# Modulation columns of the first layer's MLP: the context vector's dot products by GpSimd and ScalarE instead of VectorE

## The chip, the cores and the metric

The kernel runs on one core of a Trainium2 chip. The metric is device time in microseconds (us) of one execution; three runs of the kernel before gave 3952.34 to 3956.1, median 3953.94. TensorE multiplies matrices, VectorE (DVE), ScalarE (ACT) and GpSimd (POOL) work elementwise, and SyncE (SP) issues all DMAs. Each engine takes its instructions strictly in the order of the built program; semaphores make one engine wait for another.

## The reference, cut to what matters

Two layers of a diffusion backbone work on 1024 latent tokens and 256 context tokens of 1024 features. Each layer has a modulation: six times 1024 values for the latent tokens from the vector `c`, and six times 1024 for the context tokens from `c_ctx`, with the same weights.

```
sc, scc = silu(c), silu(c_ctx)
mod   = sc  @ w_ada[i] + b_ada[i]     # sh1, sc1, g1, sh2, sc2, g2, 1024 each
mod_c = scc @ w_ada[i] + b_ada[i]     # the same six for the context
...
x  = x  + g2  * squared_relu_mlp(modulate(x,  norm2_g, sh2,  sc2),  w_ff1, w_ff2)
xc = xc + cg2 * squared_relu_mlp(modulate(xc, norm2_g, csh2, csc2), w_ff1, w_ff2)
```

`squared_relu_mlp(h)` is `square(relu(h @ w_ff1)) @ w_ff2` with 4096 hidden features. The last layer computes no context output, so its context modulation beyond shift and scale of the first norm is not needed.

## The kernel before

Features lie on the 128 partitions, tokens along the free axis, in three blocks: block 0 is the context (256 tokens), blocks 1 and 2 the latent tokens (512 each). A weight [128, 1024] is loaded in float32 by `wload` (L296 on) and split into a high part (`whi`, ScalarE cast, L307) and its remainder (`wlo`, GpSimd subtraction, L308); every product is three matmuls (`mm3`, L313 to L315). Three such weights are held at a time.

The MLP of stage 3 is a loop over 16 steps, `fi` from 0 to 15, of two hidden tiles each. A step first makes six hidden tiles (`ff1`: matmuls into `fps`; `relu` and its square `ah` on ScalarE, L1290 and L1291; the square again in full precision on GpSimd, L1292; the remainder `al` on VectorE, L1293), then 24 output tiles (`ff2`: matmuls into `f2ps`; VectorE adds them to the residual times the gate `g2`, L1304). The gate for block 0 is that of the context. In step 0 the output tiles of block 0 come first. Matmul results share six PSUM banks, and a bank is free when ScalarE (`fps`) or VectorE (`f2ps`) has read it.

Beside the first layer's MLP the kernel computes the modulation that is still missing: column tile `m` (128 of the 6144 values, one per partition) is a dot product of a [128, 1024] piece of `w_adaT` with `silu(c)`, held on all partitions (`scr0`), and for some columns with `silu(c_ctx)` too (`scr1`). `ada_tile` (L257) does it in two halves: it loads a weight tile `adaw` of [128, 512] (256 KB, three buffers) and, for each vector, runs one VectorE instruction that multiplies and sums along the row (`adaj`, L272, followed by a short one that reads the accumulator). Step 0 lists the eight columns of `g2` of this layer (m = 40 to 47, both vectors); steps 1 to 12 list four columns each of the next layer (m = 0 to 47; both vectors up to m = 15, that is in steps 1 to 4). That is 112 weight tiles: 48 wanted for both vectors, then 64 for one, 160 VectorE instructions. A scheduler orders each engine's instructions when the program is built; it puts these tiles well ahead of the steps that list them.

`ada_tile` knows another way for vectors in its argument `other`: GpSimd multiplies (`adap`, L267, two buffers), ScalarE sums along the row into a table `part` (L268), and after eight columns `ada_sum` (L276) adds the two halves and the bias on VectorE (L279, L280). Earlier in stage 3, beside the output projection, eight columns take that way for the context vector.

Of the kernel before, what the change touches and what calls it, by code (L numbers as in the profile page):

```python
# [46 lines left out]
# columns of the constant table  # L47
C_ID, C_M0, C_M1, C_ONE, C_W = 0, 128, 256, 384, 512
# and the part of it that is needed once
# [24 lines left out]
def host_layout(inp):  # L74
    a = {k: np.asarray(v) for k, v in inp.items()}
    o = {}
    o["xT"] = np.concatenate([a["ctx"][0], a["x"][0]], 0).T.reshape(KD, P, NT).transpose(1, 0, 2)
    cc = np.stack([a["c"][0], a["c_ctx"]], 0)
    o["ccT"] = cc.reshape(2, KD, P).transpose(2, 1, 0)
    o["w_ada0"] = a["w_ada"][0, :, :2 * D]  # L80
    o["w_adaT"] = a["w_ada"].transpose(0, 2, 1)
    vec = [a["b_ada"].reshape(L * 48, P), a["norm1_g"].reshape(L * KD, P), a["norm2_g"].reshape(L * KD, P),
           a["final_norm_g"].reshape(KD, P)]
    o["vec"] = np.concatenate(vec, 0).T
    o["qag"] = a["q_a_g"].reshape(L, 2, P).transpose(0, 2, 1)
    o["kvg"] = a["kv_a_g"].reshape(L, P, 1)
    w = a["w_in"]
    q_a, kv_a, k_r, qkv, z, aa, bb = np.split(w, np.cumsum([256, 128, 32, 1536, 512, 8]), axis=-1)
    pad, pad2 = np.zeros((L, D, 48), np.float32), np.zeros((L, D, 16), np.float32)
    misc = np.concatenate([aa, bb, pad, k_r[..., :16], pad2, k_r[..., 16:], pad2], -1)  # L90
    # tiles of output columns: q 4, k 4, v 4, misc, kv_a, q_a 2, z 4
    cols = np.concatenate([qkv, misc, kv_a, q_a, z], -1)
    o["w_in"] = cols.reshape(L, KD, P, W_MT, P).transpose(0, 3, 2, 1, 4).reshape(L, W_MT, P, D)
    wq = a["w_q_b"].reshape(L, 256, H_A, DQK)
    nope = wq[..., :64].reshape(L, 256, 512)
    # the rotary columns: first halves of all heads, second halves of all heads
    pe = wq[..., 64:].reshape(L, 256, H_A, 2, 16).transpose(0, 1, 3, 2, 4)
    wq = np.concatenate([nope, pe.reshape(L, 256, 256)], -1)
    o["w_qb"] = wq.reshape(L, 2, P, QB).transpose(0, 2, 1, 3).reshape(L, P, 2 * QB)
    wk = a["w_kv_b"].reshape(L, P, H_A, 128)  # L100
    o["w_kvb"] = np.concatenate([wk[..., :64].reshape(L, P, 512), wk[..., 64:].reshape(L, P, 512)], -1)
    o["conv_w"] = a["conv_w"].reshape(L, 5, 12, P).transpose(0, 3, 2, 1).reshape(L, P, 60)
    o["a_log"] = a["a_log"].reshape(L, 8)
    o["dt_bias"] = a["dt_bias"].reshape(L, 8)
    o["gng"] = a["gdn_norm_g"].reshape(L, P, 1)
    o["w_out"] = a["w_out"].reshape(L, KD, P, KD, P).transpose(0, 3, 2, 1, 4).reshape(L, KD, P, D)
    o["w_ff1"] = a["w_ff1"].reshape(L, KD, P, 32, P).transpose(0, 3, 2, 1, 4).reshape(L, 32, P, D)
    o["w_ff2"] = a["w_ff2"].reshape(L, 32, P, D)
    tab, rope = host_constants()
    o["ctab"] = tab  # L110
    o["rope"] = rope
    return {k: np.ascontiguousarray(v) for k, v in o.items()}
# [3 lines left out]
class K:  # L116
# [13 lines left out]
    # ---------------------------------------------------------------- set-up  # L130
# [24 lines left out]
    def side(self, l):  # L155
        """The ends of the memory for the features and weights, and for the rest; layers swap them."""
        self.msd, self.osd = ("right", "left") if l % 2 else ("left", "right")
# [8 lines left out]
    def start(self, mmp, pjp, tpp, stp):  # L166
        """Modulation of the first norm, the first norm, and the first two output tiles, as the features come."""
        nc, io, cst = self.nc, self.io, self.cst
        with ExitStack() as es:
# [12 lines left out]
            # features and weights are queued behind the modulation's weights  # L182
# [10 lines left out]
            behind = START  # L193
# [62 lines left out]
    # ---------------------------------------------------------------- adaLN  # L256
    def ada_tile(self, l, m, vs, sp, width, other=()):  # L257
        """Column m of the modulation; the vectors in other go by way of Pool and ACT and want their sum()."""
# [17 lines left out]
    def ada_sum(self, l, v, m):  # L276
        """Eight columns that came by way of Pool and ACT, from their halves and the bias."""
# [4 lines left out]
    def load_sc(self, sp):  # L282
        """silu(c) and silu(c_ctx) on all partitions."""
# [6 lines left out]
    def gain(self, l, j, vs):  # L290
        """(1 + scale) * gain of norm j."""
# [5 lines left out]
    # ---------------------------------------------------------------- weights  # L297
    def wload(self, src):
        """A [128, 1024] weight from DRAM as its float32r high part and exact remainder."""
# [17 lines left out]
    # ---------------------------------------------------------------- norms  # L317
    def rstat(self, sq, n, denom, stp, rbp=None):
        """rsqrt(mean + eps) over partitions of the [128, n] squares (list added), as PSUM [128, n] rows."""
# [17 lines left out]
    def norm_mod(self, xs, rb, b, l, which, pool):  # L337
        """Modulated RMSNorm of block b (8 tiles [128, n]) into the high and low parts of h."""
# [22 lines left out]
    # ---------------------------------------------------------------- stage 1  # L361
    def stage1(self, l, last):
        """Input projection, short conv, gates, chunk preparation, latent attention's projections."""
# [8 lines left out]
        # the solves may go on into the next stage  # L372
# [59 lines left out]
        def conv_tile(m, blocks, it=None):  # L432
            """Projection, short conv, twice the silu."""
# [65 lines left out]
        def first():  # L499
            """The first two output tiles, side by side, while the norm goes on."""  # L500
# [72 lines left out]
    def kpe(self, l, it, sp, tpp):  # L573
        """Rotary key part of all heads, and the gate columns by token."""
# [40 lines left out]
    def gates(self, l, stp):  # L615
        """Per-token scalars of both directions, [128 tokens, direction, tile, head]."""
# [45 lines left out]
        # the squares are of twice the features  # L662
# [24 lines left out]
    # ---- latent attention's low-rank parts  # L687
# [6 lines left out]
    def lowrank(self, raw, b, g, sp, stp):  # L694
        """RMSNorm of the low-rank features of block b, as high and low parts."""
# [27 lines left out]
    def kv_proj(self, l, raw, sp, mmp, stp):  # L723
        """Keys (but for the rotary part) and values of all heads, to DRAM as high and low parts."""
# [20 lines left out]
    def q_proj(self, l, raw, sp, mmp, stp):  # L745
# [3 lines left out]
        # the scale of the scores  # L749
# [31 lines left out]
    # ---------------------------------------------------------------- stage 2  # L781
    def stage2(self, l, last):
        dr = self.dr
        es = ExitStack()
        # what the first scores need, and then the first steps, lies where the stage before ends first
# [4 lines left out]
        # the first scores wait for the products before them, not for the last transposes' banks  # L790
# [26 lines left out]
    def attention(self, l, last, ap, psA, psO):  # L817
# [4 lines left out]
        def parts(hi, lo, src):  # L822
            """Loads [p, n] or [p, t, n] values as their high and low parts."""
# [29 lines left out]
        # two units' results share a bank  # L853
# [3 lines left out]
        def front(h, b, half):  # L857
# [18 lines left out]
            def keep(i, c, s, c0, c1):  # L876
                """Takes scores out of their bank, with their maximum."""
# [3 lines left out]
            # the last 256 keys of both query tiles share a bank  # L881
# [18 lines left out]
            # by way of memory, to lie along the queries in all partitions  # L900
# [58 lines left out]
    def delta(self, l, last, gp, psG):  # L959
# [8 lines left out]
        # zero but for the blocks that each step fills  # L968
# [21 lines left out]
        def inverse(s):  # L990
            """The step's unit-triangular inverses, transposed, of both directions side by side: the blocks that they
            miss at each level lie in other rows and columns, so one product gives all of them."""
            U = [Ut[d, s % 2] for d in range(2)]
            B = Bt[s % 2].rearrange("p h (k j) -> p h k j", j=32)
            # at a level, direction d takes columns of blocks 2 i + d to rows of blocks 2 i + 1 - d; products of 32
            # lie in the four quarters of one of 64, a row group's right factor in the half of its parity
# [7 lines left out]
            def block(d, g, inv):  # L1004
                """Diagonal block g of the inverse (inv) or of its transpose."""
# [156 lines left out]
    # ---------------------------------------------------------------- stage 3  # L1162
    def stage3(self, l, last):
# [48 lines left out]
        for m0 in range(0, KD, 2):  # L1212
            # the last two tiles go block by block, so that the norm of a block runs beside the next one's products
# [31 lines left out]
        if not last:  # L1245
            adp = ad.enter_context(self.pool(f"ad_{l}", side=self.osd))
            self.load_sc(adp)
            ada = [(0, m, range(2)) for m in range(40, 48)] if l == 0 else []
            ada += [(l + 1, m, range(2 if m < 16 else 1)) for m in range(48)]
        # the pieces of the last products and of the norm after them  # L1250
# [28 lines left out]
        def ff1(w, b, cols=None):  # L1279
            """Squared relu of one tile, as high and low parts, by the given columns."""  # L1280
# [26 lines left out]
        for fi in range(nf):  # L1307
# [6 lines left out]
            # the last of them waits until the first block's end is under way  # L1314
# [4 lines left out]
            for a in ada[8 * fi:8 * fi + 8] if fi == 0 else ada[4 * fi + 4:4 * fi + 8]:  # L1319
                self.ada_tile(*a, adp, 512)  # L1320
# [37 lines left out]
class NormAcc:  # L1358
    """Running elementwise sum of the squares of [128, n] tiles."""
# [17 lines left out]
class Prep:  # L1377
    """Chunk preparation of the delta rule: decayed grams and inverses of the diagonal 32-blocks."""
# [57 lines left out]
    def a_view(self, d, s):  # L1436
        """The gram of a step, [row, head, column]; heads lie one block diagonal apart."""
# [3 lines left out]
    def solve(self, bi, sp):  # L1441
        """Unit-triangular inverses of the diagonal blocks of some steps, one block to a partition."""
# [4 lines left out]
        # lb[j, i] is the block's element (i, j); direction 1 holds it the other way round  # L1447
# [20 lines left out]
        # by step, head and row: blocks of the two directions in turn, each and its transpose  # L1468
# [23 lines left out]
```

## Time and profile before

| | |
|---|---|
| runs (three) | 3952.34, 3953.94, 3956.1 us |
| profiled execution, first to last instruction (span) | 3929.9 us |
| what lies around the span, against the median | 24.0 us |
| TensorE busy | 3517.4 us, 90% |
| VectorE busy | 2134.2 us, 54% |
| ScalarE busy | 1459.3 us, 37% |
| GpSimd busy | 1516.0 us, 39% |

The profiled execution's own time is given as its span alone; the time of a run has launch and end around it. Busy times are unions over the whole span, so a share says little of one stage: the MLP of the first layer runs from about 1245 us to 2121 us, and its first four steps are where the modulation is computed. Windows below are in us from the start of the span.

### The profile page before, as it was taken

The numbers are of one execution on the slowest core, as the hardware profiler recorded it, in microseconds if no ns is written. First come the engines' busy times: TensorE is split into PE (matmuls) and PEld (weight loads), VectorE is DVE, ScalarE is ACT, GpSimd is POOL, SyncE is SP. The second block draws the span as 40 slices with busy tenths as digits, with TensorE's granted clock in tenths as the row PEclk, the third lists the DMA queues.
The fourth block names the chain that finished last, engine by engine and source line by source line (L and its number), as shares of the span: only waits on it lengthen the run. The fifth ranks groups of instructions, "written<-read, shape, count | busy, mean of one in ns | idle before, by whom it ended". The sixth has DMA issues, their size and how long they took to land.

```text
span 3929.9 us, 52618 instructions
## 1 busy us (share of the span) xinstructions
PE 3517.4 (90%) x19001; PEld 2992.1 (76%) x19001; DVE 2134.2 (54%) x4080; ACT 1459.3 (37%) x3156; POOL 1516.0 (39%) x1358
## 2 busy tenths in 40 slices
PE   8789977887887898999999978888889899999998
PEld 4668766787776777888888757767788788888887
DVE  5157855565769995333333627776667533333334
ACT  4334355565633111121112524336666531222122
POOL 3124864433354232232223313675533352333232
PEclk8899987898998899999999979989899899999999
DMA  5343465535353352111111334454653511111111
GB/s 186 91 136 116 139 149 94 112 93 95 77 199 102 129 180 81 43 44 38 38 33 43 102 94 132 144 147 109 125 101 81 132 57 46 52 51 49 44 54 54
DMA packets 335892, 372.52 MB, mean 95 GB/s; under 512 B 126849, under 2 KB 226577, under 8 KB 333969
## 3 DMA queue, kind: packets, MB, share of 16 engines
q1 hardware_dynamic: 335632, 369.18, 34.3%
q8 instruction: 149, 2.44, 0.3%
q14 instruction: 111, 0.90, 0.1%
HBM read 280.65 MB, written 88.42 MB: 94 GB/s over the span
## 4 chain that ended last, share of the span: by engine, by line
PE 57%; DVE 13%; DMA 12%; issue 5%; ACT 4%; POOL 3%; SPq 1%; POOLq 0%; DVEq 0%; ACTq 0%
PE f2ps L313 6%; PE f2ps L314 6%; PE f2ps L315 6%; PE fps L314 6%; PE fps L315 6%; PE fps L313 6%; DVE adaj L272 3%; DMA raw<-kd 3%; PE g L984 3%; PE o L916 3%; PE pt L924 2%; DVE cacc L444 2%; DVE A L1427 2%; DMA rinv<-rinv 2%; DMA adaw<-w_adaT 1%
## 5 line engine op out<-in xcount | busy, mean ns | idle before, releaser
L308 POOL TENSOR_TENSOR wlo<-wraw,whi 128x1024 fp32r<-128x1024 f32 (+1 forms) x190 | 462.3, 2441 | 1217.8 <-ACT whi L307 1217.8
L1304 DVE SCALAR_TENSOR_TENSOR x<-f2ps,mod,x 128x512 f32<-128x512 f32 (+1 forms) x648 | 440.9, 689 | 353.3 <-PE f2ps L315 353.1
L307 ACT CAST whi<-wraw 128x1024 fp32r<-128x1024 f32 (+1 forms) x190 | 195.6, 1046 | 1008.0 <-PE f2ps L314 692.7
L313 PE MATMUL f2ps<-ah,whi 128*128 128x512 f32 (+1 forms) x1296 | 474.4, 371 | 31.4 <-DVE x L1304 27.2
L314 PE MATMUL f2ps<-al,whi 128*128 128x512 f32 (+1 forms) x1296 | 478.5, 370 | 0.8 <-DVE al L1293 0.8
L313 PE MATMUL fps<-hh,whi 128*128 128x512 f32 (+1 forms) x1288 | 471.3, 368 | 8.8 <-ACT hh L351 8.8
L315 PE MATMUL f2ps<-ah,wlo 128*128 128x512 f32 (+1 forms) x1296 | 477.4, 369 | 0.0
L314 PE MATMUL fps<-hl,whi 128*128 128x512 f32 (+1 forms) x1288 | 474.1, 368 | 0.0
L315 PE MATMUL fps<-hh,wlo 128*128 128x512 f32 (+1 forms) x1288 | 472.9, 368 | 0.0
L1293 DVE TENSOR_TENSOR al<-relu,ah 128x256 fp32r<-128x256 f32 (+1 forms) x161 | 111.5, 699 | 512.9 <-POOL relu L1292 512.9
L313 PE MATMUL mm<-hh,whi 128*128 128x512 f32 (+1 forms) x880 | 333.1, 380 | 35.0 <-ACT craw L430 22.1
L314 PE MATMUL mm<-hl,whi 128*128 128x512 f32 (+1 forms) x880 | 331.4, 377 | 3.6 <-DVE hl L352 2.1
L315 PE MATMUL mm<-hh,wlo 128*128 128x512 f32 (+1 forms) x880 | 327.6, 374 | 0.8 <-POOL wlo L308 0.8
L928 DVE TENSOR_TENSOR pl<-pt,ph 128x512 fp32r<-128x512 f32 x328 | 222.2, 686 | 194.7 <-ACT ph L927 182.1
L313 PEld LDWEIGHTS f2ps<-ah,whi 128*128 128x128 f32 x1296 | 248.2, 192 | 74.4 <-DVE x L1304 29.9
L313 PEld LDWEIGHTS fps<-hh,whi 128*128 128x128 f32 x1288 | 243.7, 190 | 49.1 <-ACT hh L351 9.1
L314 PEld LDWEIGHTS f2ps<-al,whi 128*128 128x128 f32 x1296 | 248.7, 192 | 40.7 <-DVE al L1293 1.0
L315 PEld LDWEIGHTS f2ps<-ah,wlo 128*128 128x128 f32 x1296 | 248.4, 192 | 40.1
L314 PEld LDWEIGHTS fps<-hl,whi 128*128 128x128 f32 x1288 | 244.0, 189 | 40.1 <-POOL hl L357 0.3
L315 PEld LDWEIGHTS fps<-hh,wlo 128*128 128x128 f32 x1288 | 243.9, 189 | 39.8
L924 PE MATMUL pt<-ctab,p 128*128 128x128 f32 x1312 | 219.9, 287 | 32.9 <-ACT p L896 12.7
L1292 POOL TENSOR_TENSOR relu<-relu 128x256 f32<-128x256 f32 (+1 forms) x161 | 159.5, 996 | 225.2 <-ACT ah L1291 209.7
(287 smaller groups left out, 7520.6 us busy)
## 6 DMA issues: line engine op xcount, KB each, us to landing
wraw<-w_ff SPq DMA_DIRECT2D x128, 512.0 KB
adaw<-w_adaT SPq DMA_DIRECT2D x160, 256.0 KB
wraw<-w_in SPq DMA_DIRECT2D x40, 512.0 KB
QK<-QK SPq DMA_DIRECT2D x72, 256.0 KB
A<-A SPq DMA_DIRECT2D x40, 256.0 KB
v<-vtd SPq DMA_DIRECT2D x40, 256.0 KB
kt<-ktd SPq DMA_DIRECT2D x40, 256.0 KB
kT<-kTd SPq DMA_DIRECT2D x36, 256.0 KB
```

The source lines that it names most:

```text
L272: nc.vector.tensor_tensor_reduce(out=j, in0=w, in1=self.sc_b[v][:, s], op0=ALU.mult, op1=ALU.add, scale=1.0, scalar=acc if i else self.bad ...
L307: nc.scalar.copy(hi[:, :n], raw[:, :n])
L308: nc.gpsimd.tensor_tensor(lo[:, :n], raw[:, :n], hi[:, :n].bitcast(F32), op=ALU.subtract)
L313: then(mm(ps, lhsT=lh, rhs=rh, start=start, stop=False))
L314: then(mm(ps, lhsT=lh, rhs=rl, start=False, stop=False))
L315: then(mm(ps, lhsT=ll, rhs=rh, start=False, stop=stop))
L916: nc.tensor.matmul(o, lhsT=v[:, k, :], rhs=x[:, j, :], start=k == 0 and i == 0, stop=k == nkt - 1 and i == 1)
L924: self.mark = nc.tensor.transpose(tp[:, j, i * P:(i + 1) * P], pp[i][:, (k0 + j) * P:(k0 + j + 1) * P], self.ident)
L928: nc.vector.tensor_tensor(pl, tp, ph.bitcast(F32), op=ALU.subtract)
L984: nc.tensor.matmul(ps[:, h, :], lhsT=lhs[:, h, :], rhs=rhs[:, h, :], start=True, stop=True)
L1292: nc.gpsimd.tensor_tensor(r[:, :n], r[:, :n], r[:, :n], op=ALU.mult)
L1304: nc.vector.scalar_tensor_tensor(xs, ps[:, :n], g2, xs, op0=ALU.mult, op1=ALU.add)
```

## The change

In the first layer's MLP loop every column is computed with `other=(1,)`: where a column is wanted for both vectors, the context's dot products go by GpSimd (48 products of [128, 512]) and ScalarE (48 sums). After each eighth such column (m = 47, then 7 and 15 of the next layer) `ada_sum` fills eight columns of the context's modulation. The latent vector's dot products stay on VectorE. Other differences are comments.

```
@@ stage3
             w2 = [self.wload(io["w_ff2"][l, f]) for f in fs]
             for a in ada[8 * fi:8 * fi + 8] if fi == 0 else ada[4 * fi + 4:4 * fi + 8]:
-                self.ada_tile(*a, adp, 512)
+                self.ada_tile(*a, adp, 512, (1,))
+                if len(a[2]) == 2 and a[1] % 8 == 7:
+                    self.ada_sum(a[0], 1, a[1] - 7)
```

The change moves instructions. GpSimd at the beginning of the MLP, before (`relu` is the square of a hidden tile, `wlo` the remainder of a weight):

```order
L1292 TENSOR_TENSOR relu<-relu 128x256 x2
L1292 TENSOR_TENSOR relu<-relu 128x512 x2
L308 TENSOR_TENSOR wlo<-wraw,whi 128x1024 x2
L1292 TENSOR_TENSOR relu<-relu 128x512 x2
L308 TENSOR_TENSOR wlo<-wraw,whi 128x1024 x2
L1292 TENSOR_TENSOR relu<-relu 128x256
L1292 TENSOR_TENSOR relu<-relu 128x512
L308 TENSOR_TENSOR wlo<-wraw,whi 128x1024
```

And with the change (a line number behind the MLP's start is one higher, so L1293 here is L1292 above):

```order
L1293 TENSOR_TENSOR relu<-relu 128x512
L267 TENSOR_TENSOR adap<-adaw,scr_12168 128x512
L1293 TENSOR_TENSOR relu<-relu 128x512
L267 TENSOR_TENSOR adap<-adaw,scr_12168 128x512
L308 TENSOR_TENSOR wlo<-wraw,whi 128x1024 x2
L267 TENSOR_TENSOR adap<-adaw,scr_12168 128x512
L1293 TENSOR_TENSOR relu<-relu 128x512
L267 TENSOR_TENSOR adap<-adaw,scr_12168 128x512
L1293 TENSOR_TENSOR relu<-relu 128x512
L267 TENSOR_TENSOR adap<-adaw,scr_12168 128x512 x33
L308 TENSOR_TENSOR wlo<-wraw,whi 128x1024 x2
L267 TENSOR_TENSOR adap<-adaw,scr_12168 128x512 x2
```

Products 5 to 37 stand in one row ahead of the split of the weights of step 1; products 38 to 48 stand among the squares and splits of step 1.

VectorE around the first output tile of step 0, before (`mod_180` is this layer's modulation, `scr_12166` is `scr0`, `scr_12168` is `scr1`; a row without tiles reads the accumulator of the one above it):

```order
L1293 TENSOR_TENSOR al<-relu,ah 128x512
L272 ISA adaj,mod_180<-adaw,scr_12166,mod_180 128x512
L272 ISA mod_180 128x1
L272 ISA adaj,mod_180<-adaw,scr_12168,mod_180 128x512
L272 ISA mod_180 128x1
L272 ISA adaj,mod_180<-adaw,scr_12166,vec 128x512
L272 ISA mod_180 128x1
L1304 SCALAR_TENSOR_TENSOR x_11021<-f2ps,mod_180,x_11021 128x256
```

And with the change (`mod_183` is the next layer's modulation):

```order
L272 ISA adaj,mod_180<-adaw,scr_12166,mod_180 128x512
L272 ISA mod_180 128x1
L272 ISA adaj,mod_183<-adaw,scr_12166,vec 128x512
L272 ISA mod_183 128x1
L272 ISA adaj,mod_183<-adaw,scr_12166,mod_183 128x512
L272 ISA mod_183 128x1
L279 TENSOR_TENSOR mod_180<-part 128x8
L280 TENSOR_TENSOR mod_180<-mod_180,vec 128x8
L1305 SCALAR_TENSOR_TENSOR x_11021<-f2ps,mod_180,x_11021 128x256
```

The first output tile of the context stood behind the reductions of three weight tiles; it now stands behind those of 18 and behind the sum over the eight columns of `g2`. Counted in the order of VectorE, the weight tiles whose reductions stand ahead of a step's first and last output tile are:

| step | before: first, last | change: first, last |
|---|---|---|
| 0 | 3, 16 | 18, 36 |
| 1 | 30, 39 | 50, 68 |
| 2 | 58, 77 | 92, 110 |
| 3 | 101, 112 | 112, 112 |

TensorE's matmuls keep their order in the MLP. ScalarE's sums stand as the products do: 33 in one row, then the casts of the two weights of step 1, and from there on a sum mostly stands just ahead of the `relu` or square of a hidden tile.

## Rows read from the trace of the kernel before

**Rows 1.** Stretches, steps 0 to 4: length, busy PE, PEld, DVE, ACT, POOL, TensorE clock, DMA.

```profile
1245.00:1322.00 77.00, 66.42 (x313) 56.13 (x312) 68.80 (x123) 27.54 (x44) 26.33 (x20) 0.85 0.27 92
1322.00:1382.20 60.20, 55.69 (x278) 47.44 (x278) 59.41 (x123) 10.05 (x16) 15.96 (x11) 0.97 0.41 133
1382.20:1447.10 64.90, 58.01 (x291) 50.01 (x290) 61.80 (x127) 10.50 (x17) 17.60 (x11) 0.92 0.58 186
1447.10:1515.00 67.90, 57.82 (x290) 49.55 (x289) 53.48 (x101) 10.24 (x17) 17.40 (x11) 0.92 0.50 160
1515.00:1570.10 55.10, 55.10 (x290) 47.55 (x289) 19.59 (x31) 10.42 (x17) 14.80 (x11) 1.00 0.13 39
```

**Rows 2.** Waits from 1269 to 1505 us: total us, times, longest.

```profile
PE f2ps L313 <- DVE x L1304: 27.0, 7, 9.2
```

**Rows 3.** VectorE in order of time, MLP: start, duration, idle before.

```profile
1284.35 0.48 DVE L1304 SCALAR_TENSOR_TENSOR x<-f2ps,mod,x 128x256 f32<-128x256 f32 x1
...
1285.53 0.75 DVE L272 CUSTOM_DVE_ANT_0 adaj<-adaw,scr,mod 128x512 bf16<-128x512 f32 x1
1286.21 0.08 DVE L272 DVE_READ_ACCUMULATOR2_ANT mod<- 128x1 f32 x1
...
1487.95 0.87 DVE L1304 SCALAR_TENSOR_TENSOR x<-f2ps,mod,x 128x256 f32<-128x256 f32 x2
...
1514.29 0.75 DVE L1304 SCALAR_TENSOR_TENSOR x<-f2ps,mod,x 128x512 f32<-128x512 f32 x1 [0.61 <-PE f2ps L315]
```

**Rows 4.** GpSimd in order of time, beside the output projection.

```profile
1116.44 8.51 POOL L267 TENSOR_TENSOR adap<-adaw,scr 128x512 f32<-128x512 f32 x5
...
1134.17 1.29 POOL L267 TENSOR_TENSOR adap<-adaw,scr 128x512 f32<-128x512 f32 x1 [1.45 <-DMA adaw<-w_adaT]
...
1152.95 6.84 POOL L267 TENSOR_TENSOR adap<-adaw,scr 128x512 f32<-128x512 f32 x4
```

**Rows 5.** VectorE in order of time, the same stretch.

```profile
1117.07 1.65 DVE L272 CUSTOM_DVE_ANT_0 adaj<-adaw,scr,mod 128x512 bf16<-128x512 f32 x1
...
1134.23 1.77 DVE L272 CUSTOM_DVE_ANT_0 adaj<-adaw,scr,vec 128x512 bf16<-128x512 f32 x1 [2.45 <-DMA adaw<-w_adaT]
...
1161.06 0.16 DVE L279 TENSOR_TENSOR mod<-part 128x8 f32<-128x8 f32 x1
```

**Rows 6.** ScalarE: line 268, ns min/median/max; then one square and, from the page, the casts.

```profile
L268 ACT ACTIVATE adap<-adap x16: 626/632/636, 1118.4 to 1159.8; 128x512 f32<-128x512 f32 x16
L268 ACT ACTIVATION_READ_ACCUMULATOR adap<-adap x16: 183/186/189, 1118.9 to 1160.4; 128x1 f32 x16
...
1271.31 0.63 ACT L1291 ACTIVATE ah<-relu 128x512 fp32r<-128x512 f32 x1
...
L307 ACT CAST whi<-wraw 128x1024 fp32r<-128x1024 f32 (+1 forms) x190 | 195.6, 1046 | 1008.0 <-PE f2ps L314 692.7
```

**Rows 7.** GpSimd in order of time, beginning of the MLP.

```profile
1272.02 2.49 POOL L1292 TENSOR_TENSOR relu<-relu 128x512 f32<-128x512 f32 x2 [1.72 <-ACT ah L1291]
1274.47 5.59 POOL L308 TENSOR_TENSOR wlo<-wraw,whi 128x1024 fp32r<-128x1024 f32 x2
```

**Rows 8.** GpSimd groups from 1600 to 2000 us: busy us, mean ns, idle before.

```profile
L308 POOL TENSOR_TENSOR wlo<-wraw,whi 128x1024 fp32r<-128x1024 f32 x29 | 69.5, 2408 | 223.6 <-ACT whi L307 223.6
L1292 POOL TENSOR_TENSOR relu<-relu 128x512 f32<-128x512 f32 x29 | 30.4, 1048 | 62.4 <-ACT ah L1291 62.4
L1292 POOL TENSOR_TENSOR relu<-relu 128x256 f32<-128x256 f32 x14 | 8.7, 622 | 0.0
```

**Rows 9.** The chain of waits: start, us, what.

```profile
1269.19 2.96 DMA adaw<-w_adaT
```

**Rows 10.** TensorE in order of time, beginning of the MLP.

```profile
1241.70 0.79 PE L313 MATMUL fps<-hh,whi 128*128 128x256 f32 x2 [7.17 <-ACT hh L351]
...
1247.42 0.41 PE L315 MATMUL fps<-hh,wlo 128*128 128x256 f32 x1
...
1250.97 0.28 PE L313 MATMUL fps<-hh,whi 128*128 128x256 f32 x1
```

## What the change should do, predicted before its run

> **What bounds the kernel now.** I read the busy time by stretch first, because the change lies in one stage. A step of the MLP that is left alone takes 55.1 us with TensorE busy throughout (the last of [rows 1]). The first four steps, beside which the modulation is computed, take 77.0, 60.2, 64.9 and 67.9 us, 270.0 together, and VectorE is busy for 68.8, 59.4, 61.8 and 53.5 of that: some 50 us of this stretch are TensorE waiting for VectorE. The list of waits names the place: output tiles wait for a PSUM bank that VectorE has not read yet, 27.0 us in seven waits [rows 2], and the granted clock falls in these stretches [rows 1]. VectorE is late because 160 reductions stand in its order between output tiles: 0.75 us and 0.08 for the accumulator, about 0.8 us each [rows 3]. So the change takes 48 of them, about 38 us, from the engine that is late. The question is what comes in their place.
>
> **The price of a product.** Beside the output projection the same pair of instructions already runs. One product alone, after an idle wait, takes 1.29 us; rows of four and five in a row take 6.84 and 8.51 us, 1.70 each [rows 4]. The VectorE reductions beside them take 1.65 us, not 0.75 [rows 5]. The two engines hold each other up: a tile costs VectorE 1.65 + 0.08, about 1.7 us, where two reductions of its own would cost 1.60. While the products run, the change therefore frees no VectorE time, except where VectorE does something that doesn't collide. I take **1.70 us a product** in a row, since the two longest rows give it, in the very arrangement that the change makes. The lower bound is 1.43: three buffers of weight tiles, each held for a load of 2.96 us [rows 9] and a product of 1.29, make (2.96 + 1.29) / 3. The upper bound is 2.04, the 1.29 and the 0.75 one after the other.
>
> The Trainium skill, page "SBUF — State Buffer", section "Who interferes with whom", says that a VectorE instruction with two SBUF inputs and a GpSimd instruction that reads SBUF exclude each other, and that the loser blocks for the whole instruction. By that rule a tile would cost 2.04 us and the sum below would come out at 34.8 us in place of 18.4. The trace has 1.70, so they collide here without excluding each other wholly.
>
> **Step 0, first output tile.** GpSimd's part, from its two squares at 1272.02 [rows 7]: 2.49, two more squares 2 x 1.05 [rows 8], two weight splits 5.59 [rows 7], products 1 to 4 at 1.70: 1289.0. Products 5 to 16 take 20.4: 1309.4. ScalarE's sum takes 0.63 + 0.19 [rows 6]: 1310.2. VectorE has to pass the reductions of 18 tiles first (they stand ahead in the order shown above). Tile 18 uses the buffer that product 15 frees at 1307.7; load 2.96, reduction 1.7, two small additions of 0.16 [rows 5]: the first output tile is read at **1312.8**, now 1284.35 [rows 3]. Until then TensorE fills its six banks and stands still.
>
> **Step 0, the rest.** TensorE has two small and 16 large output tiles left. Large ones come every 1.36 us (0.75 + 0.61 [rows 3]); small ones, half as many columns, 0.7 us. That is 23.2 us. At the beginning of the MLP it had stood idle for 7.2 us, and the records of a small matmul are then 0.41 us long up to 1247.4 and 0.28 behind [rows 10]: some 6 us at the lower of its two clock levels (1.2 for 2.4 GHz; the mean of step 0 is 0.85 of full speed [rows 1]). I charge the same here, 3 us: 1339.0. VectorE's last output tile stands behind tile 36, whose buffer product 33 frees at 1309.4 + 17 x 1.70 = 1338.3; with 2.96, 1.7 and 0.75 it ends at **1343.7**. Now: 1322.0 [rows 1]. So +21.7.
>
> **Step 1.** Its second weight is split only behind product 37. To the square that the first output tiles need, GpSimd has 12 products (20.4), three splits (3 x 2.41) and squares 2 x 1.05 and 2 x 0.62 [rows 8]: 31.0 us. Here the products no longer stand in one row: each of the four squares waits for ScalarE to finish the sum of the product ahead (0.82) and its own square (0.63 [rows 6]), 1.4 us, and two of the splits wait for a sum and a cast (1.05), 1.9 us: +9.4. But about eight products then run alone, 8 x 0.41 less: net +6.1. That gives 1338.3 + 37.1 = 1375.4. TensorE could have gone on at 1339 + 27.5 = 1366.5 (half of 55.1), so it waits some 9 us. The first output tile stands behind tile 50, whose buffer product 47 frees 3.4 us later, 1378.8; plus 2.96 and 1.7: 1383.5. From the first to the last output tile of a step take 27.0 us, as in step 3 of now (1487.95 [rows 3] to 1515.0 [rows 1]): **1410.5**, now 1382.2, +28.3.
>
> **Step 2.** No products are left, 24 single reductions stand between the last output tile of step 1 and the first of this step (tiles 68 to 92). Step 3 of now has the same picture (77 to 101) and takes 67.9 us [rows 1]: **1478.4**, now 1447.1.
>
> **Step 3** has no reductions left ahead of its tiles: 55.1 us where now 67.9, **1533.5**, now 1515.0.
>
> Everything behind runs at TensorE's pace in both, so the sum is 21.7 + 6.6 + 3.0 - 12.8 = **+18.5 us**. The 48 sums on ScalarE (39 us) cost nothing beyond the waits counted: ScalarE is busy 10 us of a 60 us step [rows 1]. The six additions of columns are 0.16 us each. The number of loads does not change. The profiled execution spans 3929.9 us and the sum is made against it; it lies 24.0 us under the median of 3953.94, and that distance stays, so the forecast is **3972 us**.
>
> **Rivals.** *Products at the pace of the loads (no change).* If products and reductions overlap when nothing else disturbs them, a product takes 1.43 us. The same steps give 1307.8 for the first output tile, 1334.0 for the end of step 0 (+12.0), no wait for GpSimd in step 1 (its square is ready at 1357, TensorE at 1361.5; last tile 1389.2), then 67.9 and 55.1: 1512.2, that is -2.8 us, 3951. It decides by the product's pace: between -2.8 at 1.43 and +18.5 at 1.70 the sum passes zero near 1.47 and +7.9 near 1.57. For it: single products of 1.29. Against it: every row of products shows 1.70. To come out faster it would need step 2 to lose its stalls too (55.1 for 67.9, -15.6, 3938), and for that nothing speaks but the freed VectorE time.
>
> *Full exclusion (slower still).* At 2.04 us step 0 ends at 1355, the square of step 1 comes at 1391, its end at 1427, then 67.9 and 55.1: 1550, +35 us, 3989. For it: a reduction that starts with a lone product takes 1.77 us [rows 5], longer than that product; against it: the pair's 1.70. It decides from about 1.9 us a product.
>
> **Chances.** A measurement of this kernel tells 0.2%, 7.9 us, from no change. Forecast and neighbourhood (product 1.6 to 1.9): 0.65. Full exclusion, or loads that come late on top: 0.11. The pace of the loads, or half of it: 0.24, of which 0.09 faster than 0.2% and 0.15 within. So slower 0.76, same 0.15, faster 0.09. The range goes from the load-paced case, 3950, to the full exclusion, 3988; about one case in ten lies on either side.
>
> **What the profile will show.** Right: products in a row of 33 at about 1.7 us and reductions beside them at 1.65; TensorE idle for some 30 us, up to about 1313, among the first `f2ps` of step 0; the four steps at about 99, 67, 68 and 55 us; from 1533 on steps of 55.1. Wrong: a product pace of 1.5 or less; the first output tile before 1300; step 2 near 55 us.

## The result, and the profile after

The change is slower: 3976.85 us median of five runs (3970.39 to 3983.66) against 3953.94 (3948.79 to 3958.59) in five runs of the kernel before beside it. The ratio is 1.0056 [1.0040, 1.0073] (in brackets the 95% interval).

The stretches of the changed kernel, cut as in [rows 1]: 24 us ahead of the first square to the end of step 0, then steps 1 to 4. Columns: stretch, length, busy PE, PEld, DVE, ACT, POOL, granted TensorE clock, DMA share, GB/s.

```profile
1256.00:1358.20 102.20, 68.47 (x341) 59.02 (x340) 89.48 (x135) 52.80 (x116) 83.58 (x56) 0.81 0.37 118
1358.20:1423.40 65.20, 53.32 (x273) 45.98 (x272) 62.28 (x100) 18.71 (x42) 39.68 (x24) 0.92 0.53 162
1423.40:1488.60 65.20, 54.45 (x271) 46.65 (x270) 54.67 (x115) 9.50 (x14) 14.90 (x10) 0.92 0.62 202
1488.60:1543.20 54.60, 54.60 (x286) 47.05 (x285) 23.89 (x34) 10.05 (x16) 15.39 (x11) 1.00 0.13 40
1543.20:1598.30 55.10, 55.10 (x290) 47.55 (x289) 19.59 (x31) 10.42 (x17) 14.81 (x11) 1.00 0.14 39
```

Against [rows 1]: step 0 is 25.2 us longer, step 1 5.0, step 2 0.3, step 3 is 13.3 shorter; together 287.2 for 270.0 us, **+17.2**. VectorE has 48 reductions less and is busy for 230.3 us in the four steps, where it was 243.5: of the some 38 us taken from it, 13 are left. Behind step 3 every step is at TensorE's pace again, as in [rows 1].

The waits from 1280 to 1545 us of the changed kernel (total us, times, longest):

```profile
PE f2ps L313 <- DVE x L1305: 40.4, 3, 28.8
...
PE f2ps L314 <- DVE al L1294: 11.0, 2, 9.4
```

In place of seven waits for output tiles, of up to 9.2 us [rows 2], there are three, one of 28.8. In step 1 TensorE also waits 9.4 us for the low part `al` of a hidden tile, which VectorE makes from GpSimd's square. Around the long one, in order of time (start, duration, idle before and what ended it):

```profile
1294.23 1.48 PE L315 MATMUL f2ps<-ah,wlo 128*128 128x256 f32 x6
1324.51 0.58 PE L313 MATMUL f2ps<-ah,whi 128*128 128x256 f32 x1 [28.79 <-DVE x L1305]
...
1327.23 0.63 PE L313 MATMUL f2ps<-ah,whi 128*128 128x512 f32 x1
...
1329.89 0.39 PE L314 MATMUL f2ps<-al,whi 128*128 128x512 f32 x1
```

Behind the stop the records of a large matmul are 0.63 us long up to 1329 and 0.39 from then on. The granted clock (the third figure from the end of a stretch) says the same: from 1324.5 to 1329.8, behind 28.8 us of standstill, it is 0.53, about its lower level of 1.2 GHz, and from 1329.8 to 1345 it is 1.00, the upper one of 2.4 GHz.

```profile
1324.50:1329.80 5.30, 5.29 (x19) 4.76 (x20) 5.30 (x12) 2.76 (x8) 4.22 (x3) 0.53 0.32 99
1329.80:1345.00 15.20, 15.20 (x69) 12.57 (x68) 15.20 (x28) 5.80 (x16) 13.87 (x9) 1.00 0.50 156
```

What VectorE does meanwhile:

```profile
1292.18 2.85 DVE L272 CUSTOM_DVE_ANT_0 adaj<-adaw,scr,mod 128x512 bf16<-128x512 f32 x1
...
1314.78 1.05 DVE L272 CUSTOM_DVE_ANT_0 adaj<-adaw,scr,mod 128x512 bf16<-128x512 f32 x1 [0.60 <-DMA adaw<-w_adaT]
...
1322.45 1.21 DVE L279 TENSOR_TENSOR mod<-part 128x8 f32<-128x8 f32 x1
1323.69 0.17 DVE L280 TENSOR_TENSOR mod<-mod,vec 128x8 f32<-128x8 f32 x1
1323.96 2.44 DVE L1305 SCALAR_TENSOR_TENSOR x<-f2ps,mod,x 128x256 f32<-128x256 f32 x6
...
1341.38 1.11 DVE L272 CUSTOM_DVE_ANT_0 adaj<-adaw,scr,mod 128x512 bf16<-128x512 f32 x1
1342.42 0.08 DVE L272 DVE_READ_ACCUMULATOR2_ANT mod<- 128x1 f32 x1
1342.42 0.74 DVE L1305 SCALAR_TENSOR_TENSOR x<-f2ps,mod,x 128x512 f32<-128x512 f32 x1
...
1351.07 1.25 DVE L280 TENSOR_TENSOR mod<-mod,vec 128x8 f32<-128x8 f32 x1
```

And GpSimd, which it follows:

```profile
1288.92 5.55 POOL L308 TENSOR_TENSOR wlo<-wraw,whi 128x1024 fp32r<-128x1024 f32 x2
...
1296.12 1.48 POOL L1293 TENSOR_TENSOR relu<-relu 128x512 f32<-128x512 f32 x1
1297.57 1.26 POOL L267 TENSOR_TENSOR adap<-adaw,scr 128x512 f32<-128x512 f32 x1
...
1300.23 23.40 POOL L267 TENSOR_TENSOR adap<-adaw,scr 128x512 f32<-128x512 f32 x14
1324.55 4.22 POOL L267 TENSOR_TENSOR adap<-adaw,scr 128x512 f32<-128x512 f32 x3 [0.92 <-ACT adap L268]
...
1332.13 18.32 POOL L267 TENSOR_TENSOR adap<-adaw,scr 128x512 f32<-128x512 f32 x11 [0.40 <-DMA adaw<-w_adaT]
```

Fourteen products take 23.40 us, eleven 18.32: 1.67 each, while the one at 1297.57, which starts while VectorE is idle, takes 1.26. VectorE waits some 0.6 us for each weight tile and reads it in 1.05: it is at the pace of GpSimd, whose products release the three buffers. The first output tile stands behind the sum `L279` of all eight columns and is read at 1323.96, 43.8 us after the first square (1280.17). The reduction of the 18th weight tile, which starts at 1321.38 and takes 1.13, ends last ahead of that sum; ScalarE had the last of the eight columns' parts at 1321.1.

The spans differ by more than that, 3968.6 for 3929.9 us. Laid side by side, ScalarE's casts and copies of the two traces drift apart by 11 us between 640 and 1050 us and by as much again in the second layer between 2630 and 3130 us, stretches in which the change moves nothing. All eleven traces of this document show how far such stretches differ: the first square of the MLP stands between 1269.1 us (the kernel before) and 1304.3, and from the last output tile of the first layer's MLP (at 2182.0 us in before, a step later than the 2121 given above) to the end of the span it is 1747.9 us (the kernel before) to 1772.0, where no edit touches anything. The trace of before is the shortest in both. What the two spans differ by outside the four steps lies within this spread, and nothing shows it to be the change's.

### The profile page after: what moved, and what is told of

Its sections match the earlier page's. It is cut to its first block, busy times and chain, and to the rows that moved or that the text cites. A ratio compares the mean times of both kernels' runs of the same rounds, so it can differ in the third digit from the quotient of the medians.

```text
span 3968.6 us, 52740 instructions
## 1 busy us (share of the span) xinstructions
PE 3516.5 (89%) x19001; PEld 2996.0 (75%) x19001; DVE 2120.0 (53%) x3990; ACT 1492.4 (38%) x3252; POOL 1593.8 (40%) x1406
## 4 chain that ended last, share of the span: by engine, by line
PE 57%; DMA 16%; DVE 9%; issue 4%; ACT 4%; POOL 4%; SPq 1%; POOLq 0%; DVEq 0%; ACTq 0%
PE f2ps L313 6%; PE f2ps L314 6%; PE f2ps L315 6%; PE fps L314 6%; PE fps L315 6%; PE fps L313 6%; DMA raw<-kd 3%; PE g L984 3%; PE o L916 3%; DMA rinv<-rinv 2%; PE pt L924 2%; DVE adaj L272 2%; DVE A L1430 2%; DVE cacc L444 2%; PE mm L313 1%
## 5 line engine op out<-in xcount | busy, mean ns | idle before, releaser
L1293 POOL TENSOR_TENSOR relu<-relu 128x256 f32<-128x256 f32 (+1 forms) x161 | 158.9, 993 | 214.0 <-ACT ah L1292 214.0
```

The source lines that it names most:

```text
L1293: nc.gpsimd.tensor_tensor(r[:, :n], r[:, :n], r[:, :n], op=ALU.mult)
```

## The experiments

One measure serves all of them: the length of a step, from the last output tile of the step before to its own on VectorE (step 0 from GpSimd's first square of the MLP), read from each trace in order of time. The steps of before come from its one trace; steps 4 to 14 take 55.1 us in every trace, but for step 4 of the two kernels with products in it (57.3 and 57.0), and step 0 of the two that leave it as it was (next_only, spread_before) is within 0.8 us of before's. Ratios are to the kernel before on the same chip.

| kernel | step 0 | 1 | 2 | 3 | sum | to before | ratio |
|---|---|---|---|---|---|---|---|
| before | 52.8 | 60.4 | 64.8 | 68.0 | 245.9 | | |
| the change | 78.1 | 65.1 | 65.2 | 54.6 | 263.1 | +17.2 | 1.0056 [1.0040, 1.0073] |
| after_again | 78.7 | 65.3 | 66.0 | 55.1 | 265.1 | +19.2 | 1.0052 [1.0033, 1.0072] |
| gate_only | 72.2 | 60.9 | 65.3 | 58.0 | 256.4 | +10.5 | 1.0042 [1.0028, 1.0056] |
| next_only | 53.1 | 68.5 | 69.7 | 64.4 | 255.7 | +9.8 | 1.0026 [1.0005, 1.0048] |
| ctx_last | 51.6 | 71.5 | 69.1 | 61.8 | 254.0 | +8.1 | 1.0036 [1.0022, 1.0050] |
| alone | 65.1 | 64.1 | 67.9 | 52.0 | 249.2 | +3.3 | one run, 3981.08 us |
| spread_before | 52.0 | 53.8 | 55.1 | 55.1 | 216.1 | -29.8 | 0.9924 [0.9907, 0.9941] |
| spread_after | 68.3 | 56.4 | 56.7 | 57.6 | 239.1 | -6.8 | 0.9985 [0.9973, 0.9997] |
| spread_ctx | 48.8 | 57.0 | 56.6 | 56.5 | 218.9 | -27.0 | 0.9941 [0.9921, 0.9961] |
| spread_before_ctx | 53.9 | 47.5 | 55.1 | 55.1 | 211.6 | -34.3 | 0.9896 [0.9865, 0.9926] |

The theory: the first output tile, gated by GpSimd, costs step 0 its time, and the products collide with VectorE, so that the stall of steps 1 and 2 stays. The rival: the products of the next layer's columns alone do it, by holding up squares and splits.

**Step 0's columns alone** (gate_only).

```
-                self.ada_tile(*a, adp, 512, (1,))
+                self.ada_tile(*a, adp, 512, (1,) if a[0] == l else ())
```

> Only the eight columns of step 0 (this layer's g2) go by GpSimd and ScalarE, 16 products; the next layer's columns are on VectorE as before. Counted from the first square of the MLP on GpSimd, steps 0 to 3 took 52.8, 60.3, 64.9 and 67.9 us before (245.9) and 78.0, 65.2, 65.2 and 54.6 with the change (263.0, +17). Theory (the first output tiles wait for the sum over eight columns, and VectorE gains nothing because products and reductions collide): the first output tile comes 43 us after the first square as with the change (15 before), step 0 takes about 71, the others 62, 66 and 57, together 256, that is +10 us or 0.25% on the whole. Rival 1 (the row of 33 products ahead of the weight split of step 1 is what costs): the row is 12 products now, step 0 near 55, nothing lost, 246. Rival 2 (each product costs the same wherever it stands): a third of 17, +6.

256.4 us, as expected. The ratio is larger than the 10.5 us, 0.26%, of the four steps: its interval begins at 0.28%, and what the rest is stays open. The gate is there with 16 products out of 48, TensorE in order of time:

```profile
1338.56 0.58 PE L313 MATMUL f2ps<-ah,whi 128*128 128x256 f32 x1 [27.97 <-DVE x L1305]
```

**The next layer's columns alone** (next_only): the same line with `a[0] > l`.

> Only the next layer's 16 columns for both vectors go by GpSimd and ScalarE, 32 products; step 0's eight columns are on VectorE as before. Theory: step 0 as before, 53 us. In step 1 the squares of the hidden tiles stand among 16 products and the last output tile stands behind weight tile 47 (39 before), so it takes about 75; then 47 to 71 tiles ahead of step 2 and 90 to 112 ahead of step 3 give 68 and 66: together 262, +16 us or 0.4%. Rival (the gate of the context in step 0 is the whole loss): with it gone all that is left is VectorE relieved of 32 reductions, 26 us: steps 1 to 3 lose their stalls, 240 or less, faster than before.

TensorE's waits in the four steps, and the last line that of the kernel before:

```profile
PE f2ps L313 <- DVE x L1305: 23.9, 7, 6.1
PE f2ps L314 <- DVE al L1294: 12.9, 3, 7.7
...
PE f2ps L314 <- DVE al L1293: 0.8, 1, 0.8
```

The gate is gone: the first output tile is at 15.2 us as before, and no wait is over 8 us. But 9.8 us are lost all the same, in step 1 above all: the waits for output tiles stand at 23.9 us against 27.0 [rows 2], and those for `al`, 0.8 us in the kernel before, come on top. That is less than the 16 expected: step 1 takes 68.5, not 75. The two halves together make 10.5 + 9.8 = 20.3 us, about the whole change. So neither the gate nor the products of the next layer's columns are the whole: each alone costs about half.

**The context's tiles last in step 0** (ctx_last), with all products kept.

```
-            for b, c in ... [(b, slice(0, BLOCKS[b][1])) for b in blocks]:
+            for b, c in ... [(b, slice(0, BLOCKS[b][1])) for b in (blocks if fi or last else [1, 2, 0])]:
```

> The change, with one more edit: in step 0 the output tiles of the context block come after those of the two latent blocks, so that they need the sum over eight columns last. Theory: the wait for the sum is covered by the 16 large output tiles, step 0 ends some 49 us after the first square (52.8 before, 78.0 with the change), but VectorE still passes 112 weight tiles at 1.7 us a pair and 1.4 and more a single one, and the stall moves on: step 1 about 78 (weight tiles 18 to 49), step 2 about 68, step 3 about 64: 259, +13 us. Rival (the gate alone): 246 or less, no slower than before.

Step 0 falls to 51.6 us and nothing is won: steps 1 to 3 take 202.4 for 193.2 of before. The stall has moved on to where the products now stand; TensorE's waits in the four steps:

```profile
PE f2ps L313 <- DVE x L1305: 25.6, 10, 6.6
PE f2ps L314 <- DVE al L1294: 15.1, 5, 9.4
```

The total, 254.0, is 5 us under the one expected, as step 1 came out at 71.5 and not at 78.

**Products without reductions** (alone): VectorE's 48 reductions of the same tiles are left out, and the latent vector's columns are copied from the context's.

> The change, but VectorE's 48 reductions of the latent vector in the columns wanted for both are left out; the latent tokens take the context's values there, so the output is another. GpSimd's products then run without VectorE reading beside them. If VectorE and GpSimd hold each other up at SBUF, a product in a row falls from 1.67 us to the pace of its loads, about 1.43, or to 1.29 if the loads keep ahead; the first output tile comes 36 us after the first square (43.8 with the change). If 1.67 is GpSimd's own pace for products in a row, or ScalarE's sum sets it, it stays 1.67 and the first output tile stays near 43. If the two exclude each other wholly (2.04 was expected then) the change could not have shown 1.67 at all.

GpSimd of this kernel in order of time:

```profile
1317.10 1.26 POOL L267 TENSOR_TENSOR adap<-adaw,scr 128x512 f32<-128x512 f32 x1 [0.43 <-DMA adaw<-w_adaT]
1318.61 1.26 POOL L267 TENSOR_TENSOR adap<-adaw,scr 128x512 f32<-128x512 f32 x1 [0.25 <-DMA adaw<-w_adaT]
1320.29 2.49 POOL L267 TENSOR_TENSOR adap<-adaw,scr 128x512 f32<-128x512 f32 x2 [0.42 <-DMA adaw<-w_adaT]
```

Without reductions beside them 44 of the 48 products take 1.25 to 1.30 us, in a row too, and the pace is that of the loads, 1.5 us. The 1.67 are made by the reductions. The first output tile still waits until 37.0 us, now for the sum alone (VectorE's wait for ScalarE's parts, total us, times, longest):

```profile
DVE mod L281 <- ACT adap L268: 19.1, 2, 16.2
```

So the collision is worth 7 us of the gate, and the rest is GpSimd's own time for its squares, splits and 16 products. The last sentence of the expectation doesn't hold: 1.67 us a pair is what whole exclusion costs here, as the section on the hardware shows; 2.04 was a wrong price for it.

**The same work later** (spread_before, spread_after). In the kernel before the weight tiles of later steps are read as early as buffers come free, 112 of them in steps 0 to 3. Of their 160 reductions 75 stand between the first and the last output tile of a step, the others ahead of a step's first output tile, among its hidden tiles. Here the loads of step `fi` are queued on SP behind that step's last `w2`, 8 tiles a step from step 1 on.

```
-        nc.sync.dma_start(raw[:, :n], src)
+        self.wld = nc.sync.dma_start(raw[:, :n], src)
...
-                self.ada_tile(*a, adp, 512)
+                with ExitStack() as q:
+                    if fi:
+                        q.enter_context(self.tc.issue_after(self.wld.ins))
+                    self.ada_tile(*a, adp, 512)
```

> The kernel before, with one thing changed: from step 1 on the loads of a step's modulation weights are queued on SP behind that step's last w2 load. Of the reductions of the 112 weight tiles, 16 reductions of 8 tiles then stand in each step from 1 to 12 on VectorE, among its hidden tiles, and none between its output tiles. The collision theory (the steps of the kernel before are long only where reductions stand between output tiles, as VectorE is then the late one) expects step 0 as before, about 53 us from the first square on, and steps 1 to 3 at 55 to 56 us where the kernel before has 60, 65 and 68: steps 0 to 3 some 219 us for 246, later steps at 55 to 56, and the whole kernel 0.5 to 0.7% faster. The rival, that VectorE is simply short of time in the MLP for 160 reductions wherever they stand, expects the 26 us to turn up in steps 1 to 12, some 2 us in each, and the same total.

Stretches of spread_before, columns as above:

```profile
1275.50:1351.70 76.20, 65.44 (x312) 55.30 (x312) 68.14 (x122) 27.56 (x44) 26.17 (x20) 0.86 0.27 83
1351.70:1405.60 53.90, 53.90 (x281) 46.35 (x280) 34.68 (x63) 10.08 (x16) 14.70 (x11) 1.00 0.25 79
1405.60:1460.70 55.10, 55.10 (x291) 47.56 (x290) 34.45 (x62) 10.42 (x17) 15.94 (x11) 1.00 0.24 77
1460.70:1515.80 55.10, 55.10 (x291) 47.55 (x290) 34.45 (x62) 10.43 (x17) 15.96 (x11) 1.00 0.24 77
```

Steps 1 to 3 are wholly TensorE's at full clock (granted 1.00), VectorE is busy for 34 us of 55, and the later steps stay at 55.1. Over the whole loop VectorE is not short of time. This alone is worth 0.76%.

The edit does two things at once: steps 1 to 4 have 16 reductions each (steps 5 to 12 eight, and not 16 as expected), where steps 1 to 3 of before have 46, 47 and 35; and all of them stand ahead of the step's first output tile, where before 18, 19 and 11 stand between output tiles. In steps 1 and 2 of before the number alone is too much: some 37 us of reductions (0.8 each) and the 19.6 us for which VectorE is busy in a step without any [rows 1] are more than 55.1. In step 3 they make only some 48 us, and it still takes 68.0, so there it is also where they stand. No run separates the two.

> The change, with the same later queueing of the modulation weights (8 products of GpSimd and 8 sums of ScalarE a step from step 1 on). If step 0's cost is the gate alone (the context's first output tile waits for all eight columns of g2 from GpSimd), step 0 stays long: first output tile at about 42 us behind the first square and the step's end at about 68. Steps 1 to 3 should fall to 55 to 58, the four together to about 236, 15 us more than in spread_before. If the products slow the MLP wherever they stand (ScalarE's sums ahead of squares), steps 1 to 3 stay above 60 and the four exceed 250.

The gate stays, 41.4 us to the first output tile and 68.3 for step 0 (TensorE's waits, the longest 26.4 us):

```profile
PE f2ps L313 <- DVE x L1305: 30.3, 4, 26.4
```

Steps 1 to 4 take 56.4 to 57.6, not 55.1. The change costs 23.0 us against spread_before in the four steps: 16.3 in step 0, about the 15 expected for the gate, and 6.7 in steps 1 to 3 beside the products.

**Both edits on the change** (spread_ctx), **and both on the kernel before** (spread_before_ctx).

> The change with both edits: the later queueing, and in step 0 the context's output tiles behind those of the latent blocks. Nothing waits for GpSimd at the start any more and nothing moves into steps 1 to 3: step 0 about 52 us, steps 1 to 3 at 55 to 58, the four together about 219, and the kernel level with spread_before within 0.1%. If GpSimd and ScalarE give VectorE real relief, it is faster than spread_before by up to 0.2%; if the products disturb, slower by 0.1 to 0.3%.

> spread_before (no products on GpSimd) with the context's output tiles last in step 0. It asks where the 3 us come from by which step 0 of spread_ctx (48.8) is shorter than that of spread_before (52.0). If from the order of the tiles alone (TensorE does not start on the small context tiles and its clock is not set back), step 0 is 49 here too, steps 1 to 3 stay at 54 to 55, the four about 213 (spread_before 216), and the ratio 0.9915 to 0.9925. If from GpSimd's relief of VectorE, step 0 stays at 51 to 52.

Stretches of spread_ctx, steps 1 and 2:

```profile
1340.30:1397.30 57.00, 55.28 (x289) 47.53 (x289) 37.33 (x47) 15.65 (x33) 29.96 (x19) 1.00 0.24 74
1397.30:1453.90 56.60, 55.35 (x290) 47.60 (x289) 37.56 (x49) 15.44 (x33) 29.62 (x19) 1.00 0.25 75
```

and of spread_before_ctx, steps 0 to 2:

```profile
1264.10:1342.20 78.10, 69.23 (x343) 57.43 (x343) 72.49 (x123) 28.44 (x47) 30.93 (x22) 0.96 0.30 96
1342.20:1389.70 47.50, 47.50 (x249) 40.95 (x248) 34.36 (x63) 9.27 (x14) 11.93 (x8) 1.00 0.22 65
1389.70:1444.80 55.10, 55.10 (x291) 47.56 (x290) 34.46 (x62) 10.42 (x17) 15.91 (x11) 1.00 0.24 77
```

In step 1 and step 2 VectorE is busier with 8 reductions beside products (37.3 and 37.6) than with 16 of its own (34.4 and 34.5). With the same order of tiles on TensorE and nothing gated, the products still cost 218.9 - 211.6 = 7.3 us in four steps and 1.9 in step 4 (57.0 for 55.1). TensorE's waits for a bank in the four steps, of spread_ctx and then of spread_before_ctx, show most of it:

```profile
PE f2ps L313 <- DVE x L1305: 13.4, 11, 1.9
...
PE f2ps L313 <- DVE x L1304: 6.9, 4, 4.2
```

The result fits neither half of the last expectation as it stands, since step 0 of spread_before_ctx is 53.9, not 49 and not 51 to 52: VectorE reads the step's last output tile late, when TensorE is already in step 1. Counted on TensorE, the last matmul of step 0's output tiles ends 50.0 us behind the first square in spread_before, 48.0 in spread_ctx and 45.5 in spread_before_ctx. So the order alone gives 4.5 us, and the products take 2.5 of them back; GpSimd gives no relief. The granted clock of the stretch of step 0 goes from 0.86 in spread_before to 0.96 in spread_before_ctx. spread_ctx is slower than spread_before by 0.17%, with intervals that overlap, and 2.8 us longer in the four steps. spread_before_ctx is the fastest of all: 3931.36 us against 3973.5 for the kernel before beside it, 1.04% [0.74, 1.35], more than the 0.75 to 0.85 expected, which lies in the interval.

**The change again** (after_again), on the chip of spread_before, spread_after and spread_ctx.

> The change itself, unedited, on the chip on which the three kernels above run. If the 17 us in the MLP are what the change costs, and the 11 us ahead of the MLP in its first profile are spread between executions, its ratio to the kernel before is 1.004 to 1.005 (17 of 3960) and the four steps take 263 us, with the time ahead of the MLP level with before's. If it also costs time elsewhere, the ratio is 1.006 or more.

The four steps take 265.1 us and the ratio is 1.0052, of which 19.2 us in the MLP are 1.0048. The MLP's first square stands at 1298.7 us, in spread_before, which has the code of the kernel before up to there, at 1299.7. In its first profile the change had it at 1280.2 and the kernel before at 1269.1. So the 11 us ahead of the MLP are spread between executions and chips, and not the change's. The ratio lies just above the 1.004 to 1.005 expected and below the 1.006 of a cost elsewhere; its interval [1.0033, 1.0072] excludes neither.

## Why the prediction held

3972 us were predicted, 3950 to 3988; 3976.85 were measured, and the four steps gave +17.2 (+19.2 in after_again) where the sum had +18.5. The two places and the two prices that carry the sum were right: the gate on the first output tile, the stall that stays, 1.70 us a product and no gain for VectorE beside it. That the sum came out within 1.3 us is partly luck: against before, step 0 cost 3.5 us more than forecast, and steps 1 to 3 cost 1.6, 2.7 and 0.5 less. Step by step, counted from the first square:

- **The first output tile**: 1312.8 less 1269.1 makes 43.7 us, measured 43.8 and 44.1. The product's pace was 1.67 for 1.70. Two errors hide in the agreement: the reduction of tile 18 ended at 42.3 us and not at 43.3, and the two additions behind it took 1.21 + 0.17 us for 2 x 0.16. gate_only and ctx_last show that this tile is what holds step 0; alone shows that the pace comes from VectorE, as taken from [rows 4, 5]. The 3 us charged for the clock behind the stop are 2.5 in the trace (5.3 us at 0.53).
- **The end of step 0**: predicted 74.6, measured 78.1. Product 33 ended at 70.3 (predicted 69.2), and from there it took 7.8 us where 5.4 were forecast for a load, a reduction and an output tile. The path was another: from the first output tile to the last of step 0 VectorE has no idle time above 0.1 us, so its own row sets the end and not the load of tile 36. In that row a term was mis-sized: the additions of columns were put at 0.16 us [rows 5], and the second pair took 0.58 + 1.25.
- **Step 1**: 66.8 predicted, 65.1 measured. The size held, the working did not. I had squares and splits wait for ScalarE (9.4 us) and about eight lone products at 1.29. GpSimd has no idle time at all from 1357.3 to 1394.0. Instead most of it is slower beside VectorE: eight of the last eleven products 1.71 to 1.75, the four large squares 1.2 to 1.5 for 1.05 [rows 8], three of four splits 2.8 for 2.4. From the end of product 33 to the square that the first output tiles need it took 34.0 us, 2.2 of them idle, where 37.1 were forecast. The two errors offset each other in part. In next_only the forecast missed by more: 75 was expected, 68.5 came.
- **Steps 2 and 3**: 67.9 and 55.1 predicted, 65.2 and 54.6 measured. Step 2 keeps its stall, with 24 single reductions ahead of its first output tile and 18 more ahead of its last; step 3 has two left.
- **Who is late, and why**: TensorE's waits for VectorE are not some 50 us of the 270.0. By [rows 1] TensorE is idle for 32 us of them; the rest of the difference to four steps of 55.1 is in part the lower clock. And not all 160 reductions stand between output tiles, only 75 do, by the order of the trace.
- **VectorE gains nothing while products run**: the balance was right (a tile at about 1.7 us), the picture of it was not. Reductions were to take 1.65 beside products; in the row they take about 1.1. Of the 1.67 us only 1.1 are the longer reduction; some 0.55 are a wait for a weight tile whose buffer the slower GpSimd still holds. In the second half of step 0 an output tile of 0.74 fills that gap, and the two engines go in lockstep at 1.70.
- **The median**: the 24.0 us between the span of before and its median were said to stay. They don't lie around a span: the execution of the change that was profiled took 3970.39 us for a span of 3968.6. With as little around it, the profiled execution of before took about 3932 us, less than any of the five beside the change (3948.79 and more). It did no harm, since the sum is a difference; the two medians differ by 22.9 us, and the interval of their ratio, 16 to 29 us, holds the 17.2 of the four steps.

Of the rivals, the pace of the loads exists, 1.5 us in alone, but only without the reductions beside it. Full exclusion had the wrong price, and the prediction was wrong to count the 1.70 against it. [rows 4, 5] show it already: the lone product at 1134.17 ends at 1135.46, and the reduction that started 0.06 us behind it ends at 1136.00, 0.54 later. So the reduction waited for all of the product, and a pair in turn costs less than the sum of the two lone times (shown in the last section). The forecast did not suffer, as its 1.70 was read from such pairs.

## What to carry to other kernels

Work handed to another engine is free only if nothing stands behind it in the order and if the engine that was relieved does not share memory access with the new one: price the pair from a place where both run side by side, never from a lone instruction. And before moving work off an engine that is late, look at where it stands: queueing the same reductions later, at most 16 to a step and away from the output tiles, left VectorE 20 us of every 55 to spare and won 30 us, where moving 48 of the 160 to GpSimd lost 17 to 19.

## What the runs showed of the hardware

VectorE's reductions and GpSimd's instructions run by turns, each waiting for the whole of the other. Three GpSimd instructions of the changed kernel, one by one, to be read against the reductions at 1292.18 and 1314.78 shown above:

```profile
1291.67 2.81 POOL L308 TENSOR_TENSOR wlo<-wraw,whi 128x1024 fp32r<-128x1024 f32 x1
...
1313.59 1.71 POOL L267 TENSOR_TENSOR adap<-adaw,scr 128x512 f32<-128x512 f32 x1
...
1315.26 1.71 POOL L267 TENSOR_TENSOR adap<-adaw,scr 128x512 f32<-128x512 f32 x1
```

The split ends at 1294.48 and the reduction that started beside it at 1295.03; the product ends at 1315.30 and the reduction at 1315.83; the next product ends 1.13 us behind that reduction. It is always so: in the four steps of the changed kernel 47 reductions start while a product or a split runs, and 46 of them end 0.55 us behind it (one of these behind the split that followed the product at once), the last 0.68; the 39 products that start while a reduction runs end 1.12 to 1.17 us behind it. A reduction alone takes 0.75 and a product 1.26, so 0.2 and 0.1 us of each pass during the wait. By turns a pair takes 0.55 + 1.12 = 1.67 us, the pace of the row, and not the 2.01 of the lone times. Beside a product a reduction mostly takes about 1.1 us (37 of them, median 1.11), beside a split 2.2 to 2.9 (nine of ten, median of all ten 2.75), by how much of the other was left when it started. The output tiles, which read one operand from PSUM, took 0.74 beside products and 0.75 without them [rows 3]. The Trainium skill, page "SBUF — State Buffer", section "Who interferes with whom", has a VectorE instruction with two SBUF inputs contend with a GpSimd one that reads SBUF, one with at most one SBUF input and outside the 2-port modes not, and the loser of the shared ports blocked for the whole instruction. The traces agree on who contends and on the wait for the whole instruction, with the 0.55 and 1.12 us above; lone times added up overstate what it costs.

A VectorE addition over 128x8 elements, 0.16 us alone [rows 5], took 1.21 and 1.25 beside products: each ended 0.02 us behind the product that ran when it started. So a short instruction pays for the long one beside it.
